# Seven half-size block products in place of eight, in both matrix products of the MLP

## The chip, the cores and the metric

The kernel runs on one core of a Trainium2 chip. The metric is device time in microseconds (us). The five engines work side by side, each through a queue of its own: PE (TensorE) multiplies matrices, DVE (VectorE), ACT (ScalarE) and POOL (GpSimd) work on elements, SP (SyncE) issues all DMAs of this kernel.

## The reference, cut to what matters

Two layers stand one after the other; each is a mixer and an MLP, with norms around both. x is 1024 tokens by 1024 features in float32.

```python
def rmsnorm(x, w, eps=1e-6):
    return x * rsqrt(mean(x * x, axis=-1, keepdims=True) + eps) * w

for layer in range(2):
    x = x + rmsnorm(mixer(rmsnorm(x, mix_pre[layer])), mix_post[layer])
    u = rmsnorm(x, mlp_pre[layer])
    h = square(relu(u @ mlp_w_up[layer]))            # 1024 x 1024 by 1024 x 4096
    x = x + rmsnorm(h @ mlp_w_down[layer], mlp_post[layer])   # 1024 x 4096 by 4096 x 1024
```

Layer 0 mixes by a gated delta rule and an RWKV-7 recurrence, layer 1 by chunkwise retention; the change leaves both mixers as they are.

## The kernel before

A float32 operand of a product is kept as an exact pair of float32r parts, hi = a cast of it on ACT and lo = the rest, by a subtraction on DVE or POOL (`split_w`, `split_act`). A block product is then three matmuls: hi by hi, lo by hi, hi by lo. All matmuls go through `mm` (L178); those of the MLP stream 512 columns each.

`mlp` works in three stages. In the first (L1187 to L1210 and L1252 to L1258), `normed(t)` does the norms for token tile t of 128 tokens: `post_norm` (a load of the residual, `rms`, a POOL product with the norm's weights at L250, a DVE step at L252), then `pre_norm` (`rms` again, L259) and the transposes on PE (L265), whose results are split into the pair `us[hf]` of a half of 512 tokens. `mlp` is a generator: its first steps run between the last products of the mixer. `upward` (L1214) makes feature tiles of the hidden layer, with all of the first half first: 24 matmuls into one PSUM bank for each half and tile, then relu and square on ACT and DVE into hi and lo, which stay in SBUF. So the first half's products can run while the second half's norms are still under way. `downward` (L1233) multiplies two or four of these tiles with their rows of the second weights, 8 token tiles by 2 column halves, and DVE adds each bank to the sum `facc` (L1248). The main loop alternates the two: 15 turns, each of two feature tiles up and two down. At the end, the last `downward` goes token tile by token tile with four feature tiles each, and `finish(t)` does the closing norms of a tile (and, in layer 0, those of the next mixer's input) behind it.

SBUF is cut by hand into pieces (`region((a, b))` in kilobytes; a new use of a piece waits for the end of the old). A ring of buffers (`area(n)`) holds n tiles of a name. The order on each engine is set by the order of the code and by a scheduler's clock; what it gave is quoted with the change.

## Time and profile before

| | |
|---|---|
| time, median of 3 runs | 3415.32 us (3414.01 to 3421.27) |
| the profiled execution: its span | 3408.8 us, which is 6.5 us under the median |
| PE busy in the span | 3265.6 us (96%), 17192 matmuls |
| DVE, ACT, POOL busy | 1845.1 (54%), 1053.1 (31%), 682.8 us (20%) |
| mean granted clock of PE | 0.957 of full speed |

The profile gives no time of its own for the profiled execution beside its span, so the span and the 6.5 us around it stand for it. A busy time is a sum over stages with different limits. Stage by stage it reads otherwise: in the mixers every engine works in turns, and in the MLPs PE has hardly a gap. The views used below are the page's summary; the busy time of each engine by stretch of the span; the groups of instructions by line and shape; and the instructions of one engine in order of time, with the wait before them in brackets.

### The profile page before, as it was taken

The numbers are of one execution on the slowest core, as the hardware profiler recorded it, in microseconds if no ns is written. First come the engines' busy times: TensorE is split into PE (matmuls) and PEld (weight loads), VectorE is DVE, ScalarE is ACT, GpSimd is POOL, SyncE is SP. The second block draws the span as 40 slices with busy tenths as digits, with TensorE's granted clock in tenths as the row PEclk, the third lists the DMA queues.
The fourth block names the chain that finished last, engine by engine and source line by source line (L and its number), as shares of the span: only waits on it lengthen the run. The fifth ranks groups of instructions, "written<-read, shape, count | busy, mean of one in ns | idle before, by whom it ended". The sixth has DMA issues, their size and how long they took to land.

```text
span 3408.8 us, 44062 instructions
## 1 busy us (share of the span) xinstructions
PE 3265.6 (96%) x17192; PEld 2789.7 (82%) x17192; DVE 1845.1 (54%) x3539; ACT 1053.1 (31%) x1972; POOL 682.8 (20%) x1217
## 2 busy tenths in 40 slices
PE   8899899999898899999999999999999999999998
PEld 6677788778777788888887899988999888888887
DVE  6445555555544634444448665667656734444445
ACT  5332333232232421121214343234433432222122
POOL 1663364446320200000003101112011200000002
PEclk9898899898696999999999999999999999999999
DMA  5221222121242511111115322344223411111112
GB/s 164 65 62 42 67 71 70 50 68 51 58 146 76 190 45 49 44 49 45 45 48 177 89 85 83 93 128 127 83 85 99 155 44 50 50 50 50 50 50 99
DMA packets 340562, 268.49 MB, mean 79 GB/s; under 512 B 63232, under 2 KB 305792, under 8 KB 340352
## 3 DMA queue, kind: packets, MB, share of 16 engines
q1 hardware_dynamic: 340352, 265.67, 25.9%
q8 instruction: 135, 2.21, 0.3%
q14 instruction: 75, 0.61, 0.1%
HBM read 230.49 MB, written 35.13 MB: 78 GB/s over the span
## 4 chain that ended last, share of the span: by engine, by line
PE 74%; DMA 7%; DVE 7%; POOL 6%; issue 2%; ACT 2%; SPq 1%; DVEq 0%; POOLq 0%; ACTq 0%
PE bank L178 73%; POOL piece L617 3%; POOL piece L613 3%; DMA piece<-dm 2%; DMA dx<-piece 1%; DVE piece L252 1%; DVE piece L198 1%; ACT piece L233 1%; DVE mt L239 1%; DMA piece<-dx 1%; DMA piece<-h 1%; DVE piece L259 1%; DMA piece<-ud 0%; DMA piece<-yd 0%; DVE piece L1248 0%
## 5 line engine op out<-in xcount | busy, mean ns | idle before, releaser
L178 PE MATMUL bank<-piece,piece 128*128 128x512 f32 (+7 forms) x16176 | 3156.1, 357 | 78.9 <-ACT piece L305 15.1
L178 PEld LDWEIGHTS bank<-piece,piece 128*128 128x128 f32 (+1 forms) x16176 | 2666.3, 196 | 530.6 <-issue 33.6
L1248 DVE TENSOR_TENSOR piece<-piece,bank 128x512 f32<-128x512 f32 x448 | 307.1, 686 | 523.0 <-PE bank L178 521.1
L198 DVE TENSOR_TENSOR piece<-piece,piece 128x1024 fp32r<-128x1024 f32 x322 | 406.7, 1263 | 261.2 <-ACT piece L197 253.9
L197 ACT CAST piece<-piece 128x1024 fp32r<-128x1024 f32 x332 | 347.8, 1048 | 477.4 <-PE bank L178 383.4
L250 POOL TENSOR_TENSOR piece<-piece,piece 128x1024 f32<-128x1024 f32 x32 | 81.2, 2539 | 1618.1 <-DVE piece L1248 1329.4
L1225 ACT ACTIVATE piece<-bank 128x512 f32<-128x512 f32 x128 | 76.3, 596 | 735.2 <-PE bank L178 735.2
L613 POOL TENSOR_TENSOR piece<-piece 128x120 f32<-128x120 f32 (+22 forms) x496 | 182.7, 368 | 219.5 <-DMA piece<-dm 184.0
L617 POOL TENSOR_TENSOR piece<-piece,piece 128x120 f32<-128x120 f32 (+22 forms) x496 | 194.5, 392 | 37.4
L1331 POOL TENSOR_TENSOR piece<-piece,piece 128x512 f32<-128x512 f32 x32 | 64.1, 2004 | 521.7 <-DVE piece L1330 467.2
L305 ACT CAST piece<-piece 128x256 fp32r<-128x256 f32 (+3 forms) x122 | 65.9, 545 | 174.9 <-DVE piece L1500 40.2
L1227 DVE TENSOR_TENSOR piece<-piece 128x512 f32<-128x512 f32 x128 | 89.8, 702 | 52.6 <-ACT piece L1226 52.5
L306 DVE TENSOR_TENSOR piece<-piece,piece 128x256 fp32r<-128x256 f32 (+3 forms) x122 | 82.6, 684 | 53.2 <-ACT piece L305 39.2
L233 ACT ACTIVATE piece<-piece 128x1024 f32<-128x1024 f32 (+1 forms) x64 | 67.7, 1057 | 110.0 <-DVE piece L1248 56.1
L1226 ACT ACTIVATE piece<-piece 128x512 fp32r<-128x512 f32 x128 | 80.9, 632 | 47.1 <-PE bank L178 44.9
L1228 DVE TENSOR_TENSOR piece<-piece,piece 128x512 fp32r<-128x512 f32 x128 | 90.1, 704 | 1.6
L178 PE MATMUL bank<-piece 64*128 64x128 f32 (+1 forms) x384 | 61.3, 315 | 9.1 <-DVE piece L979 7.1
L660 DVE COPY_PREDICATED piece<-piece,bank 128x384 f32<-128x384 uint32 (+2 forms) x96 | 41.9, 440 | 51.8 <-PE bank L178 51.4
L265 PE MATMUL bank<-ident,piece 128*128 128x128 f32 x256 | 41.1, 306 | 28.7 <-DVE piece L259 24.6
L178 PEld LDWEIGHTS bank<-piece 64*128 64x128 f32 (+1 forms) x384 | 53.0, 216 | 17.1 <-DVE piece L979 8.6
L638 DVE STREAM_TRANSPOSE piece<-piece 128x256 f32<-128x256 f32 x16 | 7.1, 445 | 107.4 <-DMA piece<-dx 96.8
L265 PEld LDWEIGHTS bank<-ident,piece 128*128 128x128 f32 x256 | 34.0, 158 | 36.4 <-DVE piece L259 26.5
(191 smaller groups left out, 1713.7 us busy)
## 6 DMA issues: line engine op xcount, KB each, us to landing
piece<-in_ret_w_in_dram SPq DMA_DIRECT2D x96, 512.0 KB
piece<-in_mlp_w_up_dram SPq DMA_DIRECT2D x64, 512.0 KB
piece<-in_mlp_w_down_dram SPq DMA_DIRECT2D x64, 512.0 KB
piece<-in_ab_w_in_dram SPq DMA_DIRECT2D x60, 512.0 KB
piece<-in_ret_w_out_dram SPq DMA_DIRECT2D x32, 512.0 KB
h<-piece SPq DMA_DIRECT2D x24, 512.0 KB
piece<-h SPq DMA_DIRECT2D x24, 512.0 KB
piece<-in_x_dram SPq DMA_DIRECT2D x16, 512.0 KB
```

Source lines behind the costliest of these rows:

```text
L178: PE.matmul(ps, lhsT, rhs, start=start, stop=stop)
L197: ACT.copy(hi, raw)
L198: eng.tensor_tensor(out=lo, in0=raw, in1=hi, op=ALU.subtract)
L233: ACT.activation(junk, xt, AF.Square, accum_out=ss)
L250: POOL.tensor_tensor(out=u, in0=f, in1=wb, op=ALU.mult)
L306: DVE.tensor_tensor(out=lo, in0=y, in1=hi, op=ALU.subtract)
L613: POOL.tensor_tensor(out=t, in0=Mb[:, j : j + 1, j + 1 : 32].to_broadcast([P, c, n]), in1=X[:, 0:c, j : j + 1].to_broadcast([P, c, n]), op ...
L617: POOL.tensor_tensor(out=X[:, 0:c, j + 1 : 32], in0=X[:, 0:c, j + 1 : 32], in1=t, op=ALU.subtract)
L1226: ACT.activation(hH[:, sl], r, AF.Square)
L1227: DVE.tensor_tensor(out=r, in0=r, in1=r, op=ALU.mult)
L1228: DVE.tensor_tensor(out=hL[:, sl], in0=r, in1=hH[:, sl], op=ALU.subtract)
L1248: DVE.tensor_tensor(out=dstf, in0=dstf, in1=ps, op=ALU.add)
```

## The change

Both products of each MLP are done by the Strassen-Winograd scheme. Each operand is cut in four blocks, sums of blocks are formed, seven block products are made, and their sums give the four blocks of the result.

Upward (16 steps p per layer, each for two feature tiles): the blocks of the weights are a11, a12, a21, a22 (feature tile by half of the 1024 inputs), those of the normed input b11, b21 (first token half) and b12, b22 (second). t1 = b12 - b11, t2 = b22 - t1, t3 = b22 - b12, t4 = b21 - t2 are formed once, in `combine(t)`, as the second half's transposes come out. Each step forms four sums of the weights on POOL, splits seven operands, and makes seven products of 12 matmuls. Where two products go into a sum together, the second is added to the first in its PSUM bank, so a step uses four banks. Relu is on ACT, the square on POOL, and the squared tile goes to DRAM (`store`).

Downward (4 quarters c of the hidden layer per layer, 7 products n each, two steps s to a product): the raw blocks of hidden layer and weights are loaded (`fetch`), POOL forms the sums (`prepare`), ACT and DVE split them into a ring of three, PE makes 24 matmuls a step into four banks, and `flush` adds a bank to one of seven accumulators (ACT copies it in quarter 0). In quarter 3, `combined` adds the accumulators into `facc`, and `end` starts the closing norms behind the last two products.

```diff
@@ first stage: the second half's operands
+                def sink(g, ps):
...
+                    if g == 0:
+                        ts["b12"] = mk(tp, sh, "b12")
+                        ts["t1"] = mk(tmp, sh, "t1")
+                        ACT.copy(ts["b12"], ps)
+                        DVE.tensor_tensor(out=ts["t1"], in0=ps, in1=b11[0][:, :, tt], op=ALU.subtract)
+                        DVE.tensor_tensor(out=ts["t1"], in0=ts["t1"], in1=b11[1][:, :, tt], op=ALU.subtract)
+                        put("t1", ts["t1"], DVE)
+                        return
...
+                    DVE.tensor_tensor(out=ts["t2"], in0=ps, in1=ts["t1"], op=ALU.subtract)
+                    DVE.tensor_tensor(out=ts["t3"], in0=ps, in1=ts["b12"], op=ALU.subtract)
+                    put("b22", ps, DVE)
+                    put("t2", ts["t2"], DVE)
+                    POOL.tensor_tensor(out=ts["t4"], in0=b21[0][:, :, tt], in1=ts["t2"], op=ALU.subtract)
+                    put("t3", ts["t3"], POOL)
+                    POOL.tensor_tensor(out=ts["t4"], in0=ts["t4"], in1=b21[1][:, :, tt], op=ALU.add)
+                    put("t4", ts["t4"], POOL)
@@ upward
-            def upward(*tiles, between=()):
...
+            raws = region((0, 16)).area(2)
+            def product(ps, w, u, start, stop):
+                for k in range(4):
+                    PE.matmul(ps, w[0][:, k, :], u[0][:, k, :], start=start and k == 0, stop=False, skip_group_check=True)
+                    PE.matmul(ps, w[0][:, k, :], u[1][:, k, :], start=False, stop=False, skip_group_check=True)
+                    PE.matmul(ps, w[1][:, k, :], u[0][:, k, :], start=False, stop=stop and k == 3, skip_group_check=True)
+            def store(p, f, t, r):
+                POOL.tensor_tensor(out=r, in0=r, in1=r, op=ALU.mult)
+                SP.dma_start(hd[p // 4][f, t][:, p % 4, :], r)
...
+            parts = [first_part(p, begun[p][0], begun[p][1], begun[p][2], keep) for p in range(2)]
+            for p in range(2):
+                second_part(p, parts[p][0], begun[p][2], keep)
+            for p in range(16):
...
+                POOL.tensor_tensor(out=S[:, 0], in0=q["a21"], in1=q["a22"], op=ALU.add)
+                POOL.tensor_tensor(out=S[:, 1], in0=S[:, 0], in1=q["a11"], op=ALU.subtract)
+                POOL.tensor_tensor(out=S[:, 2], in0=q["a11"], in1=q["a21"], op=ALU.subtract)
+                POOL.tensor_tensor(out=S[:, 3], in0=q["a12"], in1=S[:, 1], op=ALU.subtract)
+                b6 = mk(psu, [P, HT], "pu")
+                product(b6, operand(S[:, 1]), ops["t2"], True, True)
+                u2 = mk(us_, [P, HT], "u2")
+                DVE.tensor_tensor(out=u2, in0=x1, in1=b6, op=ALU.add)
...
@@ downward
-            def downward(i0, hs, after=None):
...
+            half = region((24, 32)).area(1)
+            ring = region((104, 136), (40, 56)).area(3)
+            def prepare(n, s, v):
+                if n == 7:
+                    a, b = mk(half, sh, "s3"), mk(half, sh, "t3")
+                    plus(POOL, a, v["a11"], v["a21"], ALU.subtract)
+                    plus(POOL, b, v["b22"], v["b12"], ALU.subtract)
+                elif n == 5:
+                    a, b = v["a21"], v["b12"]
+                    plus(POOL, a, a, v["a22"])
+                    plus(POOL, b, b, v["b11"], ALU.subtract)
+                elif n == 6:
+                    a, b = v["a21"], v["b12"]
+                    plus(POOL, a, a, v["a11"], ALU.subtract)
+                    plus(POOL, b, v["b22"], b, ALU.subtract)
+                elif n == 3:
+                    a, b = v["a12"], v["b22"]
+                    plus(POOL, a, a, v["a21"], ALU.subtract)
+                elif n == 4:
+                    a, b = v["a22"], v["b12"]
+                    plus(POOL, b, b, v["b21"], ALU.subtract)
...
+                return split_in(ring, sh, a, "a"), split_in(ring, sh, b, "b")
+            def combined(n):
+                for t in range(4):
+                    v = {k: x[t] for k, x in acc.items()}
+                    if n == 7:
+                        plus(POOL, v[4], v[7], v[4], ALU.subtract)
+                    elif n == 1:
+                        plus(POOL, v[2], v[2], v[1])
+                    elif n == 5:
+                        plus(POOL, v[3], v[3], v[5])
+                        plus(POOL, v[5], v[5], v[7])
+                    elif n == 6:
+                        plus(DVE, v[1], v[1], v[6])
+                        plus(DVE, v[3], v[3], v[1])
+                        plus(DVE, v[4], v[4], v[1])
+                        plus(POOL, v[5], v[5], v[1])
+            order = (7, 1, 5, 6, 2, 3, 4)
```

Three places show how the instructions now stand. In the names, the number behind `piece` is where the buffer lies in kilobytes, and the number behind `bank` is the PSUM bank.

PE, layer 0, around the last transposes of the first stage (`L265` before, `L267` after). Before:

```order
L178 MATMUL bank6_7_75<-piece164_40_7660,piece40_53_7977 128x512
L178 MATMUL bank6_7_75<-piece148_38_7658,piece56_55_7979 128x512
L265 MATMUL bank2_3_71<-ident_59_127,piece72_51_7706 128x128 x4
L265 MATMUL bank3_4_72<-ident_59_127,piece72_51_7706 128x128 x4
L265 MATMUL bank1_2_70<-ident_59_127,piece72_51_7706 128x128 x4
L178 MATMUL bank4_5_73<-piece172_41_7661,piece88_46_7669 128x512
L178 MATMUL bank5_6_74<-piece172_41_7661,piece40_53_7977 128x512
L178 MATMUL bank0_1_69<-piece172_41_7661,piece48_54_7978 128x512
L265 MATMUL bank2_3_71<-ident_59_127,piece72_51_7706 128x128 x4
```

After, with the first and the last two of the eight groups of transposes:

```order
L1290 MATMUL bank1_2_70<-piece164_40_7676,piece40_48_7996 128x512
L1291 MATMUL bank1_2_70<-piece156_39_7675,piece56_50_7998 128x512
L267 MATMUL bank3_4_72<-ident_75_143,piece172_43_7681 128x128 x4
L267 MATMUL bank2_3_71<-ident_75_143,piece172_43_7681 128x128 x4
...
L267 MATMUL bank2_3_71<-ident_75_143,piece172_43_7681 128x128 x4
L1289 MATMUL bank6_7_75<-piece104_52_8013,piece48_49_7997 128x512
L1290 MATMUL bank6_7_75<-piece112_53_8014,piece48_49_7997 128x512
L1291 MATMUL bank6_7_75<-piece104_52_8013,piece64_51_7999 128x512
```

Before, the second half's transposes stand among the first half's products; now all eight groups stand together behind the 48 matmuls of the two early products of p = 0 and 1, and the next product (with t2, piece 104) stands behind all of them.

POOL, layer 0, the same place: L250 and L1178 are the norms' product with their weights, L198 the split of weights, L1248, L1250 and L1227 the work of `combine` on t3 (piece 196) and t4 (piece 24, piece 96), L1298 a square, L1338 and L1340 the first sums of weights. Before:

```order
L250 TENSOR_TENSOR piece120_50_7677<-piece104_47_7672,piece196_45_7665 128x1024 x4
L198 TENSOR_TENSOR piece56_55_7979<-piece36_8_151,piece40_53_7977 128x1024
L250 TENSOR_TENSOR piece120_50_7677<-piece104_47_7672,piece196_45_7665 128x1024 x2
L198 TENSOR_TENSOR piece64_56_7980<-piece36_8_151,piece48_54_7978 128x1024
L198 TENSOR_TENSOR piece88_46_7669<-piece32_7_150,piece88_46_7669 128x1024
L250 TENSOR_TENSOR piece120_50_7677<-piece104_47_7672,piece196_45_7665 128x1024 x2
```

After:

```order
L1178 TENSOR_TENSOR piece172_43_7681<-piece172_43_7681,piece32_41_7677 128x1024 x6
L1298 TENSOR_TENSOR piece16_63_8184<-piece16_63_8184 128x512 x2
L1248 TENSOR_TENSOR piece24_62_8023<-piece156_39_7675,piece24_62_8023 128x512
L1250 TENSOR_TENSOR piece24_62_8023<-piece24_62_8023,piece164_40_7676 128x512
L1227 TENSOR_TENSOR piece196_57_8018<-piece24_62_8023,piece188_56_8017 128x4x128
L1178 TENSOR_TENSOR piece172_43_7681<-piece172_43_7681,piece32_41_7677 128x1024
L1227 TENSOR_TENSOR piece96_61_8022<-piece24_62_8023,piece88_60_8021 128x4x128
...
L1227 TENSOR_TENSOR piece96_61_8022<-piece24_62_8023,piece88_60_8021 128x4x128
L1338 TENSOR_TENSOR piece24_64_8229<-piece0_46_7993 128x512
L1340 TENSOR_TENSOR piece24_64_8229<-piece0_46_7993 128x512
```

The norms of the last two token tiles now stand behind the squares of p = 0 and 1, which wait for the early products, and the first sums of weights stand behind all of `combine`, whose scratch (piece 24) they take over.

POOL, layer 0, end of the MLP: pieces 72 to 96 are `facc`, 16 and 64 accumulators 7 and 1, the 128x1024 rows `prepare`, L1178 and L250 the closing norms. Before:

```order
L198 TENSOR_TENSOR piece56_55_7979<-piece32_7_150,piece40_53_7977 128x1024
L250 TENSOR_TENSOR piece120_71_11683<-piece72_61_8328,piece104_69_11640 128x1024 x2
L250 TENSOR_TENSOR piece120_71_11683<-piece80_62_8329,piece104_69_11640 128x1024 x2
```

After:

```order
L1400 TENSOR_TENSOR piece8_71_10106<-piece8_71_10106,piece180_75_10110 128x1024 x2
L1400 TENSOR_TENSOR piece72_76_10127<-piece72_76_10127,piece88_78_10129 128x512 x2
L1400 TENSOR_TENSOR piece80_77_10128<-piece80_77_10128,piece96_79_10130 128x512 x2
L1400 TENSOR_TENSOR piece88_78_10129<-piece88_78_10129,piece16_80_10131 128x512
L1400 TENSOR_TENSOR piece164_72_10107<-piece164_72_10107,piece148_69_10104 128x1024
L1400 TENSOR_TENSOR piece88_78_10129<-piece88_78_10129,piece16_80_10131 128x512
L1400 TENSOR_TENSOR piece96_79_10130<-piece96_79_10130,piece16_80_10131 128x512 x2
L1400 TENSOR_TENSOR piece164_72_10107<-piece164_72_10107,piece148_69_10104 128x1024
L1400 TENSOR_TENSOR piece88_78_10129<-piece88_78_10129,piece64_82_10133 128x512 x2
L1400 TENSOR_TENSOR piece96_79_10130<-piece96_79_10130,piece64_82_10133 128x512 x2
L1178 TENSOR_TENSOR piece72_76_10127<-piece72_76_10127,piece0_94_11879 128x1024 x2
```

Before, POOL does nothing in the MLP but the norms at its two ends; now the sums of accumulators stand between `prepare` for product 4 and the two rows of product 3 (piece 164), which PE needs.

## Rows read from the trace of the kernel before

**Rows 1.** The page's summary: span, and busy time, share and instructions by engine.

```profile
span 3408.8 us, 44062 instructions
PE 3265.6 (96%) x17192; PEld 2789.7 (82%) x17192; DVE 1845.1 (54%) x3539; ACT 1053.1 (31%) x1972; POOL 682.8 (20%) x1217
```

**Rows 2.** Busy time (count) by engine, clock, DMA share, GB/s; one stretch per MLP.

```profile
1400.00:1500.00 100.00, 100.00 (x443) 82.87 (x442) 47.76 (x65) 21.09 (x29) 0.00 (x0) 1.00 0.20 61
3200.00:3300.00 100.00, 100.00 (x443) 82.84 (x442) 45.72 (x64) 17.63 (x24) 0.00 (x0) 1.00 0.14 43
```

**Rows 3.** ACT in order of time (start, length), the same relu one loop turn apart.

```profile
1305.14 0.60 ACT L1225 ACTIVATE piece<-bank 128x512 f32<-128x512 f32 x1 [14.72 <-PE bank L178]
...
1348.66 0.60 ACT L1225 ACTIVATE piece<-bank 128x512 f32<-128x512 f32 x1 [14.72 <-PE bank L178]
```

**Rows 4.** DVE in groups by line and shape: busy us, mean ns, idle before.

```profile
L1248 DVE TENSOR_TENSOR piece<-piece,bank 128x512 f32<-128x512 f32 x448 | 307.1, 686 | 523.0 <-PE bank L178 521.1
L1228 DVE TENSOR_TENSOR piece<-piece,piece 128x512 fp32r<-128x512 f32 x128 | 90.1, 704 | 1.6
```

**Rows 5.** DVE in order of time: a 1024-wide subtraction and a norm's step, POOL idle.

```profile
1107.73 1.22 DVE L198 TENSOR_TENSOR piece<-piece,piece 128x1024 fp32r<-128x1024 f32 x1
1108.88 1.28 DVE L252 SCALAR_TENSOR_TENSOR piece<-piece,mr,piece 128x1024 f32<-128x1024 f32 x1
```

**Rows 6.** POOL in order of time: a sum 512 wide.

```profile
1870.34 1.30 POOL L1413 TENSOR_TENSOR piece<-piece,piece 128x512 fp32r<-128x512 f32 x1 [0.73 <-ACT piece L1412]
```

**Rows 7.** ACT in groups by line and shape: casts 1024 wide.

```profile
L197 ACT CAST piece<-piece 128x1024 fp32r<-128x1024 f32 x332 | 347.8, 1048 | 477.4 <-PE bank L178 383.4 <-DMA piece<-in_mlp_w_up_dram 65.4 <-DMA piece<-in_ret_w_in_dram 9.7
```

**Rows 8.** POOL in order of time: first stage of the MLP of layer 0.

```profile
1130.96 4.76 POOL L198 TENSOR_TENSOR piece<-piece,piece 128x1024 fp32r<-128x1024 f32 x2
```

**Rows 9.** DVE in order of time, there: three steps on one column each.

```profile
1131.06 2.31 DVE L240 SCALAR_TENSOR_TENSOR mt<-mt,ms 128x1 f32<-128x1 f32 x1
1133.41 2.33 DVE L241 SCALAR_TENSOR_TENSOR mr<-mt,mr 128x1 f32<-128x1 f32 x1
...
1141.69 0.16 DVE L240 SCALAR_TENSOR_TENSOR mt<-mt,ms 128x1 f32<-128x1 f32 x1
```

**Rows 10.** POOL in order of time: a closing norm's product in layer 0.

```profile
1825.40 2.42 POOL L250 TENSOR_TENSOR piece<-piece,piece 128x1024 f32<-128x1024 f32 x1 [3.93 <-DVE piece L252]
```

**Rows 11.** DVE in order of time, there: a step that reads a PSUM bank.

```profile
1826.42 0.68 DVE L1248 TENSOR_TENSOR piece<-piece,bank 128x512 f32<-128x512 f32 x1
```

**Rows 12.** PE in order of time: first stage in layer 0, from its first longer run.

```profile
1126.95 13.24 PE L178 MATMUL bank<-piece,piece 128*128 128x512 f32 x50 [3.27 <-DVE piece L281]
...
1142.12 5.27 PE L178 MATMUL bank<-piece,piece 128*128 128x512 f32 x22
...
1151.66 6.91 PE L178 MATMUL bank<-piece,piece 128*128 128x512 f32 x22 [2.36 <-POOL piece L198]
...
1164.89 75.39 PE L178 MATMUL bank<-piece,piece 128*128 128x512 f32 x329
```

**Rows 13.** ACT in order of time: the last token tile's first norm in layer 1.

```profile
2701.79 1.06 ACT L233 ACTIVATE piece<-piece 128x1024 bf16<-128x1024 f32 x1 [2.96 <-DVE piece L1363]
```

**Rows 14.** Busy time by stretch, as rows 2: first stage and end of both MLPs.

```profile
2700.00:2720.00 20.00, 18.18 (x89) 14.87 (x88) 19.06 (x32) 11.22 (x21) 7.06 (x3) 1.00 0.54 181
2720.00:2740.00 20.00, 20.00 (x94) 16.66 (x93) 8.22 (x13) 5.89 (x10) 0.00 (x0) 1.00 0.23 79
...
3390.00:3409.00 19.00, 9.79 (x44) 7.77 (x42) 9.91 (x22) 4.33 (x9) 7.14 (x3) 0.81 0.44 166
```

**Rows 15.** The same, the turn from layer 0 to layer 1.

```profile
1800.00:1850.00 50.00, 46.85 (x221) 37.28 (x219) 45.49 (x89) 24.86 (x50) 17.35 (x7) 1.00 0.45 154
1850.00:1870.00 20.00, 16.84 (x79) 14.37 (x80) 17.38 (x34) 7.47 (x15) 7.10 (x4) 0.83 0.75 247
```

**Rows 16.** POOL in order of time: the last two closing norms of layer 1.

```profile
3395.54 2.40 POOL L250 TENSOR_TENSOR piece<-piece,piece 128x1024 f32<-128x1024 f32 x1 [3.01 <-DVE piece L1248]
3400.94 2.34 POOL L250 TENSOR_TENSOR piece<-piece,piece 128x1024 f32<-128x1024 f32 x1 [3.00 <-DVE piece L1248]
```

More of the change, by code (lines that the diff above doesn't have):

```diff
@@ L1252, in mlp @@
-            if layer == 0:
-                for t in (4, 5, 4):
-                    next(run[t])
-                steps = ((6, 5, 4), (7, 6, 5), (7, 6), (7,))
-            else:
-                steps = ((7, 6), (7,))
-            hs = upward(0, 1, 2, 3, between=steps)
-            facc = [mk(fp, [P, D], f"fa{t}") for t in range(8)]
-            downward(0, hs[:2])
-            prev = (2, hs[2:])
-            for g in range(2, 15):
-                hs = upward(2 * g) + upward(2 * g + 1)
-                downward(*prev)
-                prev = (2 * g, hs)
@@ L1281, in mlp, with quads, operand @@
-            run = [finish(t) for t in range(8)]
-            def after(t):
+            def quads(p):
+                raw = mk(raws, [P, KT, 2 * P], "raw")
+                SP.dma_start(raw, mlp_w_up[layer][:, 2 * P * p : 2 * P * (p + 1)].rearrange("(k p) c -> p k c", p=P))
+                return {f"a{f + 1}{k + 1}": raw[:, 4 * k : 4 * k + 4, P * f : P * f + P] for f in range(2) for k in range(2)}
+            def operand(src, eng=DVE):
+                return split_in(ring, [P, 4, P], src, "op", eng)
```

253 lines of the change are left out of this document (183 added, 70 removed).

## The prediction

> **What bounds the kernel now.** The summary comes first: PE is busy for 96% of the span, no other engine for more than 54% [rows 1]. That is a mean over stages, so the next view is the busy time by stretch. In the middle of either MLP, PE is busy for 100.00 of 100 us at the full granted clock, while DVE stands at 46 to 48 and ACT at 18 to 21, and POOL does nothing at all [rows 2]. The same relu comes back after 1348.66 - 1305.14 = 43.52 us [rows 3]; that is a turn of the main loop, with 96 matmuls up (two feature tiles, two halves, 24 each) and 96 down. So one matmul costs 43.52 / 192 = 0.2267 us, and in this stage every matmul less is worth that, as long as PE stays the engine that is waited for. What has to be asked is who keeps PE fed, since the three others are given more to do, and POOL most.
>
> **What the change removes.** Each MLP has 2 x 1536 matmuls before (32 feature tiles x 2 halves x 24 up; 32 x 16 x 3 down). Seven eighths are left, 2688: 16 steps x 7 x 12 = 1344 up, 4 quarters x 7 x 48 = 1344 down. Over both layers 768 matmuls go, of the same shape: 768 x 0.2267 = **-174.1 us**. The Trainium skill, on the page "TensorE: Matmul & The Clock Gate", section "Wait — 56ns, not 53.3ns?", has 215.7 ns between such matmuls, with which the term would be 165.7; the trace has 226.7 here, weight loads included, and that is used.
>
> **What it adds, and whom DVE and POOL wait for.** The new work has one price that a sum of busy times does not show. Two POOL subtractions took 4.76 us from 1130.96 on [rows 8]; in that time DVE steps on a single column, 0.16 us long at other times, took 2.31 and 2.33 us [rows 9]: each had to wait for the POOL instruction under way. Both their inputs lie in SBUF. A DVE step that reads a PSUM bank kept its 0.68 us under a POOL product [rows 10, 11]. So POOL's work on SBUF and DVE's steps with two SBUF inputs take turns, and I add them up: "the shared sum". The Trainium skill says the same, on "SBUF — State Buffer", section "Who interferes with whom": an exclusive lock, and only for DVE instructions with two SBUF inputs; by that rule the bank sums stay free, and if they did not, the last rival below would be the forecast. Prices: DVE 1.22 us for 1024 columns, 1.28 for a norm's step [rows 5], 0.70 for 512, 0.69 from a bank [rows 4]; POOL 2.40 for 1024 [rows 16], 1.30 for 512 [rows 6]; ACT 1.05 for 1024 [rows 7].
>
> *Upward, steady.* A step has 84 matmuls, 19.0 us. POOL: four sums and four squares, 8 x 1.30 = 10.4. DVE: seven splits, 4.9, and five sums from banks, 3.4. Shared sum 15.3, DVE 8.3, ACT twelve instructions of about 0.6 [rows 3], 7.2. All are under 19.0, and the ring holds six to eight operands, which is at least 16 us of PE ahead. Cost nothing; PE is the cover, and if a step became bound by the shared sum it would have to grow by 3.7 us first.
>
> *Downward, quarters 0 to 2.* A quarter has 336 matmuls, 76.2 us. POOL: 16 instructions of `prepare`, 38.4. DVE: 28 splits, 34.2; 28 flushes, 19.3 (on ACT in quarter 0). Shared sum 72.6, only 3.6 us under PE; the ring lets a split run two steps (10.9 us) ahead. Product 6 needs sums in place over product 5's, so POOL works in bursts with the splits between. I take 1.5 us of stall a quarter, six quarters: +9 (0 if the ring covers all; 5 a quarter if it does not: 0 to 30). The loads (8 MB a quarter, about 110 GB/s) are under the 181 GB/s that one 20 us stretch moved [rows 14].
>
> *Quarter 3.* `combined` adds 20 POOL sums, 26.0 us, and 12 DVE sums with both inputs in SBUF, 8.4. Shared sum 72.6 + 34.4 = 107.0, against 76.2 + 10.9 of lead. Of the 20 over, the last four POOL sums (5.2) stand behind both rows of product 3, so PE does not wait for them: 15, rounded to +16 for a layer, +32 in all (24 to 40; half of it if the order leaves more room: 16).
>
> *First stage, layer 0.* Only two of a step's seven products need the first token half alone, so PE has 4 x 12 = 48 matmuls, 10.9 us, while the second half's norms run; before it had 96, and more after them. In the quoted order all transposes of the second half stand behind the 48, and the product with t2 behind all transposes. From 1126.95 [rows 12] the 48 end at 1137.8. Then follow on POOL: two squares 2.6, the last two norms' products 4.8, 16 instructions of `combine` 20.8, three sums of weights 3.9: 32.1; and DVE's part with two SBUF inputs: 12 x 0.70 + 4 x 1.28 = 13.5. That is 45.6, with a split behind it about 47; some DVE steps will lie ahead, so the product starts at about 1180. PE idles 42 us. Before, 99 matmuls (22.4 us) stood in the 38 us from 1126.95 to where the long run sets in [rows 12], so 16 were lost already: **+26** (12 if only the last tile's own chain counts, 40 if DVE's bank steps add up with it).
>
> *First stage, layer 1.* `raws` lies at 0 to 16 KB, where the mixer's last outputs are read, so the weights of p = 0 can be loaded only after them; the last tile's norm starts at 2701.8 [rows 13], a load of 1 MB at 181 GB/s [rows 14] takes about 6, and the 48 matmuls start at about 2709. DVE then has 28 steps of `combine`, 19.3, six splits 4.2, two norm steps 2.6, and about 5 of waits for POOL, from the first transposes at 2712: the t2 product starts at about 2743. PE loses 2743 - 2701 - 11 = 31. Before, 1.8 us were idle in that time [rows 14], and by estimate 4 went to transposes: +25 (10 to 35).
>
> *Clock.* After PE's idle time at the turn of the layers, a stretch of 20 us shows a granted clock of 0.83 [rows 15], which is 3.4 us lost between the full 2.4 and 1.2 GHz. Two long idle times are new: +6 (2 to 8).
>
> *Up to down.* a11 and a21 take the place of b11, which is free 6 products, 16 us, before the end; 2 MB, and one sum and split, just fit in: +2 a layer, +4 (0 to 14).
>
> *Ends.* Before, tiles reach the closing norm 5.4 us apart [rows 16]; now the last four come within 4.1 us, and POOL and DVE need 4 x (2.40 + 1.28) = 14.7 for them. PE's 44 matmuls end at about 3400 [rows 14], 8.8 us before the end; then it would be about 16: +8 (3 to 14). At the turn to layer 1, 3.2 + 3.2 us were idle already [rows 15]; eight norms now crowd there too, each with two norm steps: +8 (0 to 20).
>
> Sum: 9 + 32 + 26 + 25 + 6 + 4 + 8 + 8 = 118 given back of 174: **-56 us**. The span of 3408.8 would become 3353, and with the 6.5 us around it, at which the profiled execution stands below the median of 3415.3, **3359 us**.
>
> **The rivals.** *A: little is given back.* The added work hides and PE stays full, as in the middle of the MLPs now [rows 2]. For it: every steady sum above is under PE's time. Against it: the quoted order puts the transposes behind the 48 matmuls. With the low ends 0 + 16 + 12 + 10 + 2 + 0 + 3 + 0 = 43: 3415 - 131 = 3284.
>
> *B: slower, because the downward half is bound by DVE and POOL together.* If POOL's bursts stop DVE in its queue so that the flushes behind a waiting split wait too, POOL and all of DVE add up: 38.4 + 34.2 + 19.3 = 91.9 in quarters 1 and 2, 15.7 over PE each; in quarter 3 126.3, 39 over PE with its lead. That is 2 x (31.4 + 39) = 141 where I have 41: 3459. It decides against the change once a quarter takes about 14 us longer than forecast in each of the four (8 x 7 = 56, with the last one double). For it: 4 to 6 us of the four flushes stand between splits; DVE is a queue in order. Against it: flushes run in just the time in which a split would wait for POOL [rows 10, 11], and product 1 and 2 have no sums at all.
>
> That the change does not do what it says is no rival: the two orders differ by exactly 768 matmuls, 15483 to 14715 PE instructions.
>
> **How the numbers follow.** Forecast, with its own range of 3305 to 3405: 0.72. A, down to 3280: 0.14. B, above 3410: 0.14. The range takes in A's middle and leaves out about half of A's tail and B: 3280 to 3410. A measurement of this kernel can tell about 0.2% from no change, so faster means below 3408.5 and slower above 3422: 0.83, 0.03 and 0.14.
>
> **What would show it.** Right: PE's matmuls are 768 fewer and a run of 336 takes 76 to 78 us in quarters 0 to 2; two gaps of 35 to 45 us at the t2 products, with DVE and POOL taking turns in them; a stall of some 15 us in quarter 3 before product 3, ended by POOL. Wrong: gaps in the upward steps; quarters over 85 us (B); the second half's operands ready within 20 us of the early products (A); a load from DRAM as the releaser of a downward step.

## The result: 3447.4 us, one per cent slower

The changed kernel takes 3447.44 us (median of four runs, 3436.65 to 3458.76), the kernel before 3418.3 in the same series: 1.0107 times as long, with an interval of 1.0066 to 1.0149. The forecast was 3359 with a range up to 3410. The profiled run of the changed kernel took 3436.65, of which 3434.9 are its span, 10.8 us under its median; its span is 26.1 us over that of before [rows 1].

Lines of the changed kernel's code have numbers of their own: L1289 to L1291 are the matmuls upward and L1491 to L1493 downward, L235 a norm's square, L1178 its product with the weight row on POOL, L1179 and L261 the last steps of the first and of the second norm, L1176 and L1180 the load and the store of a residual row, L267 the transposes, L1169 the cast and L1170 the remainder of a split, L1227 a remainder in `combine`, L1400 a sum downward.

The page's summary answers [rows 1]: 768 matmuls fewer and 151.9 us less work for PE, more than twice the work for POOL.

```profile
span 3434.9 us, 44170 instructions
PE 3113.7 (91%) x16424; PEld 2653.9 (77%) x16424; DVE 2153.4 (63%) x3555; ACT 1255.8 (37%) x2252; POOL 1498.0 (44%) x1665
```

The busy time by stretch, for the steady upward half, the closing quarter 3 of layer 0 and the first stage of layer 0 (columns as in [rows 2]):

```profile
1400.00:1500.00 100.00, 100.00 (x443) 82.81 (x442) 43.21 (x61) 37.39 (x62) 46.87 (x40) 1.00 0.36 117
...
1752.00:1850.00 98.00, 82.84 (x336) 66.34 (x334) 92.18 (x80) 32.89 (x38) 78.06 (x34) 0.90 0.10 32
...
1112.00:1219.00 107.00, 26.59 (x117) 20.35 (x116) 66.81 (x121) 41.53 (x82) 42.01 (x26) 0.60 0.39 134
```

In the middle all is as forecast: PE is full, POOL at 47% hides. In quarter 3 DVE is busy for 92 of 98 us; its waits for POOL count as busy there. In the first stage PE worked 27 of 107 us, at a mean granted clock of 0.60, and no engine was full. DVE's 66.81 and POOL's 42.01 us together would fill the 107, so this row alone does not tell a shared sum of work from a chain. The view of the chain that ended last speaks for a chain (its longest pieces: start, length, what), and e1 below decides it:

```profile
1118.13 7.96 DMA piece<-fd
1126.11 2.19 ACT piece L235 x4
1130.19 1.28 DVE piece L1179
1131.47 1.21 DVE piece L261
1132.72 1.98 PE bank L267 x8
1134.72 3.92 DMA piece<-fd
1138.66 2.19 ACT piece L235 x4
1142.74 1.28 DVE piece L1179
1144.02 1.21 DVE piece L261
1145.28 1.98 PE bank L267 x8
1147.28 3.98 DMA piece<-fd
```

A tile's transposes end, the next row of the mixer's output is loaded into the buffer that they left, then two norms, then transposes: 12.6 us a tile, one tile at a time, although the ring holds two. The 48 early matmuls start at 1159.7, 46.9 us after the mixer's last matmul (4.1 in the kernel before), the product with t2 at 1218.8 (PE in order of time):

```profile
1159.68 1.22 PE L1289 MATMUL bank<-piece,piece 128*128 128x512 f32 x2
...
1218.82 0.79 PE L1289 MATMUL bank<-piece,piece 128*128 128x512 f32 x1 [10.89 <-ACT piece L1169]
```

At the end the same: SyncE's queue in order of time, and DVE's last steps of the norms.

```profile
3399.91 2.38 SPq L1180 DMA_DIRECT2D out_dram<-piece  x2
3402.58 2.66 SPq L1176 DMA_DIRECT2D piece<-h  x2
3410.25 4.46 SPq L1180 DMA_DIRECT2D out_dram<-piece  x2
3414.81 2.84 SPq L1176 DMA_DIRECT2D piece<-h  x2
3420.52 2.16 SPq L1180 DMA_DIRECT2D out_dram<-piece  x2
3423.20 2.36 SPq L1176 DMA_DIRECT2D piece<-h  x2
3428.36 2.72 SPq L1180 DMA_DIRECT2D out_dram<-piece  x2
```

```profile
3419.21 1.28 DVE L1179 SCALAR_TENSOR_TENSOR piece<-piece,mr,piece 128x1024 f32<-128x1024 f32 x1 [1.53 <-DMA piece<-h]
...
3427.05 1.28 DVE L1179 SCALAR_TENSOR_TENSOR piece<-piece,mr,piece 128x1024 f32<-128x1024 f32 x1 [4.74 <-DMA piece<-h]
```

Two stores, two loads, two stores: a pair of residual rows is loaded only when the pair before has been stored. The last matmul ends at 3397.6, 37.3 us before the end; before it was 9.0.

**Where the time went.** A stage's loss is the time between two marks, less 0.2267 us for each matmul of an MLP in it; its excess is that minus the same in the kernel before. That kernel has no quarters; what it lost itself between its last downward matmuls, 8.5 us, is taken off at the turn, where the forecast counted it too, and the loss of quarter 3 stands in full. The marks are matmuls: the 5000th of the mixer of layer 0 (at 1066.7 before, 1066.0 after), the first of each quarter, the last downward, the 1000th and 5000th of the mixer of layer 1, and the end. Excess in us; the columns e1 to e13 are experiments told below, quarters are of both layers together:

| | forecast | changed | e1 | e2 | e3 | e5 | e8 | e13 |
|---|---|---|---|---|---|---|---|---|
| first stage, layer 0 | 26 + 3 | 68.1 | 33.2 | 68.9 | 73.4 | 33.4 | 32.4 | 28.9 |
| first stage, layer 1 | 25 + 3 | 34.4 | 35.3 | 35.3 | 33.8 | 34.1 | 38.3 | 34.6 |
| quarters 0 to 2 | 9 + 4 | 12.3 | 10.7 | 12.9 | 12.4 | 13.8 | 13.7 | 17.3 |
| quarter 3 | 32 | 43.4 | 43.9 | 42.6 | 31.4 | 28.0 | 28.3 | 25.9 |
| turn to layer 1 | 8 | 15.2 | 13.6 | 11.4 | 18.8 | 15.0 | 14.3 | 12.4 |
| end | 8 | 28.2 | 26.1 | 17.0 | 33.2 | 19.8 | 12.0 | 12.7 |

(The forecast's 6 for the clock stand with the first stages, its 4 for up to down with the quarters.) In the changed kernel that is 201.6, the mixers took 1.5 less, and -174.1 + 200.1 = +26.0 is the difference of the spans. Where an edit does not touch a stage, its loss still varies by 3 to 5 us from profile to profile. In the first stage of layer 0 that scatter lies in the end of the mixer, from its 5000th to its last matmul (44 to 51 us in the 15 profiles). From the mixer's last matmul to the product with t2 the four kernels that leave this stage as it is (changed, e2, e3, e7) take 106.0 to 107.0 us; in layer 1 the same four take 44.5 to 46.0.

### The profile page after: what moved, and what is told of

Same layout as the page of the kernel before. It is cut to its first block, busy times and chain, and to the rows that moved or that the text cites. A ratio compares the mean times of both kernels' runs of the same rounds, so it can differ in the third digit from the quotient of the medians.

```text
span 3434.9 us, 44170 instructions
## 1 busy us (share of the span) xinstructions
PE 3113.7 (91%) x16424; PEld 2653.9 (77%) x16424; DVE 2153.4 (63%) x3555; ACT 1255.8 (37%) x2252; POOL 1498.0 (44%) x1665
## 4 chain that ended last, share of the span: by engine, by line
PE 58%; DVE 12%; POOL 11%; DMA 10%; issue 5%; ACT 2%; SPq 1%; DVEq 0%; POOLq 0%; ACTq 0%
PE bank L180 33%; PE bank L1290 5%; PE bank L1291 5%; PE bank L1289 5%; POOL piece L1400 4%; POOL piece L619 3%; DVE piece L1170 3%; POOL piece L615 3%; PE bank L1492 2%; PE bank L1493 2%; PE bank L1491 2%; DVE piece L1400 2%; DMA piece<-dm 2%; DMA dx<-piece 2%; DMA piece<-h 1%
## 5 line engine op out<-in xcount | busy, mean ns | idle before, releaser
L180 PE MATMUL bank<-piece,piece 128*128 128x512 f32 (+7 forms) x10032 | 1742.2, 335 | 70.5 <-ACT piece L307 19.1
L180 PEld LDWEIGHTS bank<-piece,piece 128*128 128x128 f32 (+1 forms) x10032 | 1501.2, 199 | 279.3 <-issue 35.8
L1170 DVE TENSOR_TENSOR piece<-piece,piece 128x512 fp32r<-128x512 f32 (+1 forms) x448 | 643.3, 1454 | 190.4 <-ACT piece L1169 185.8
L1169 ACT CAST piece<-piece 128x512 fp32r<-128x512 f32 (+1 forms) x448 | 365.4, 836 | 701.1 <-PE bank L1290 248.2
L1400 POOL TENSOR_TENSOR piece<-piece,piece 128x1024 f32<-128x1024 f32 (+1 forms) x168 | 471.3, 2835 | 175.5 <-DVE piece L1170 69.0
L1492 PE MATMUL bank<-piece,piece 128*128 128x512 f32 x896 | 353.9, 395 | 30.5 <-DVE piece L1170 30.5
L1289 PE MATMUL bank<-piece,piece 128*128 128x512 f32 x896 | 351.5, 393 | 19.5 <-ACT piece L1169 16.8
L1491 PE MATMUL bank<-piece,piece 128*128 128x512 f32 x896 | 350.7, 395 | 9.1 <-ACT piece L1169 9.1
L1290 PE MATMUL bank<-piece,piece 128*128 128x512 f32 x896 | 350.5, 391 | 1.9 <-DVE piece L1227 1.9
L1493 PE MATMUL bank<-piece,piece 128*128 128x512 f32 x896 | 351.3, 393 | 0.3 <-DVE piece L1170 0.3
L1291 PE MATMUL bank<-piece,piece 128*128 128x512 f32 x896 | 350.0, 391 | 0.1
L200 DVE TENSOR_TENSOR piece<-piece,piece 128x1024 fp32r<-128x1024 f32 x202 | 261.8, 1297 | 136.4 <-ACT piece L199 133.7
L199 ACT CAST piece<-piece 128x1024 fp32r<-128x1024 f32 x204 | 213.5, 1047 | 300.0 <-PE bank L180 274.2
L1492 PEld LDWEIGHTS bank<-piece,piece 128*128 128x128 f32 x896 | 170.4, 190 | 71.7 <-DVE piece L1170 36.5
L1289 PEld LDWEIGHTS bank<-piece,piece 128*128 128x128 f32 x896 | 169.6, 189 | 56.4 <-ACT piece L1169 17.4
L1491 PEld LDWEIGHTS bank<-piece,piece 128*128 128x128 f32 x896 | 170.6, 191 | 47.2 <-ACT piece L1169 11.2
L1290 PEld LDWEIGHTS bank<-piece,piece 128*128 128x128 f32 x896 | 169.7, 189 | 37.8 <-DVE piece L1227 2.4
L1493 PEld LDWEIGHTS bank<-piece,piece 128*128 128x128 f32 x896 | 170.5, 190 | 36.0 <-DVE piece L1170 0.8
L1291 PEld LDWEIGHTS bank<-piece,piece 128*128 128x128 f32 x896 | 169.3, 189 | 36.8 <-DVE piece L1170 1.5
```

What stands on the lines that cost most here:

```text
L180: PE.matmul(ps, lhsT, rhs, start=start, stop=stop)
L1169: ACT.copy(hi, src)
L1170: eng.tensor_tensor(out=lo, in0=src, in1=hi, op=ALU.subtract)
L1289: PE.matmul(ps, w[0][:, k, :], u[0][:, k, :], start=start and k == 0, stop=False, skip_group_check=True)
L1290: PE.matmul(ps, w[0][:, k, :], u[1][:, k, :], start=False, stop=False, skip_group_check=True)
L1291: PE.matmul(ps, w[1][:, k, :], u[0][:, k, :], start=False, stop=stop and k == 3, skip_group_check=True)
```

## The experiments

**e1, buffers and order in the first stage of layer 0.**

```diff
-                nfa = region((172, 180)).area(2)
...
+                early = region((104, 120)).area(4), region((120, 136)).area(4)
+                mid_ = region((172, 180)).area(2), region((180, 188)).area(2)
+                late_ = region((56, 64)).area(2), region((64, 72)).area(2)
...
-                steps = ((0, 1, 0, 0, 2, 1), (1, 3, 2), (2, 4, 3), (3, 5), (4, 5))
+                steps = ((0, 1, 2, 3, 0, 1), (0, 1, 2, 3), (2, 3, 4), (5, 4), (6, 5))
```

> The first stage of layer 0 alone is changed: each of the eight token tiles gets a buffer of its own for the mixer's output and one for the residual rows (space that the operands of the second half take later), and the first four tiles' loads and norms are asked for before their transposes. No arithmetic is added or taken away. Theory R (rings): in the changed kernel each tile there takes 12.6 us (transposes at 1132.7, 1145.3, 1157.9) because one tile's load, norms and transposes must end before the next one's load lands, so this stage falls from 67 us over the kernel before to 25 to 35, and the run to 3400 to 3412. Theory S (shared sum of POOL and DVE): the work of both engines is what takes the time, none of it is gone, so the run stays within 8 us of 3447.

3399.2 us, ratio 0.9981 [0.9953, 1.0008]; the stage's excess falls from 68.1 to 33.2 and every other stage stays. PE in order of time shows the first half's transposes:

```profile
1110.43 1.10 PE L267 MATMUL bank<-ident,piece 128*128 128x128 f32 x8 [3.52 <-DVE piece L261]
1114.78 1.97 PE L267 MATMUL bank<-ident,piece 128*128 128x128 f32 x8 [3.25 <-DVE piece L261]
1117.09 1.12 PE L267 MATMUL bank<-ident,piece 128*128 128x128 f32 x4 [0.34 <-DVE piece L283]
1119.19 1.12 PE L267 MATMUL bank<-ident,piece 128*128 128x128 f32 x4 [0.99 <-DVE piece L283]
1124.75 1.97 PE L267 MATMUL bank<-ident,piece 128*128 128x128 f32 x8 [4.44 <-DVE piece L261]
```

Four tiles in 16 us, where it was 47 (1112.7 to 1159.9). Theory R holds: with no instruction less on PE, DVE, ACT or POOL, 35 us come back.

**e9, the order alone**, with `steps = ((0, 1, 0, 1, 0, 1), (2, 3, 2, 3), (2, 3, 4), (5, 4), (5,))` and rings of two.

> The changed kernel with the order of the first stage's steps in layer 0 changed and nothing else, rings of two as they are: tiles 0 and 1, then 2 and 3 are asked for in pairs, a tile's second norm and transposes ahead of the next pair's loads. Theory O (order): the 12.6 us a tile come from a second norm that stands behind the next tile's first in the queues of ACT and DVE, while that tile's rows wait for a free buffer; two tiles then go in 12.6 us or a little more, and the stage falls by 20 to 30 of the 35 that buffers and order together gave: ratio to the kernel before 1.001 to 1.005. Theory B (buffers): two buffers with a load of 4 us behind each pair are the limit whatever the order: the stage within 5 us of before this edit, ratio 1.008 to 1.013.

Ratio 1.0045 [1.0023, 1.0068], the stage 14 us shorter: between the theories. The ratio is what order foretold, the stage's 14 are short of its 20. From the mixer's last matmul to the product with t2 it is 91.8 us where the changed kernel has 106.0 and e1 72.5. So of the 35 this order alone gives 14, and 21 need the buffers.

**e2, more buffers for the closing norms.**

```diff
-                            nrm, rowa = region((16, 24)).area(2), region((0, 8)).area(2)
+                            rowa = region((0, 8)).area(2)
+                            nrm = region((16, 24), (56, 72), (188, 196)).area(8) if layer else region((16, 24), (64, 72)).area(4)
```

> Only the ring of residual rows in the closing norms is changed: eight buffers in layer 1 and four in layer 0 in place of two. Theory R: the last norms come in pairs 8 to 9 us apart (their steps end at 3399.8/3401.9, 3410.2/3414.3, 3420.5/3422.3, 3428.3/3430.7) because a pair's rows are loaded only after the rows of the pair before have been stored; with all rows there the end after the last matmul falls from 37 us to 15 to 20 and the turn to layer 1 gets 5 to 8 shorter: 3447 - 25 = 3415 to 3428. Theory S: four tiles times POOL's 2.4 and DVE's 1.28 and what DVE still has queued set the end: within 8 us of 3447.

Ratio 1.0039 [1.0016, 1.0062]. All eight loads are now issued before the last matmul, which ends at 3389.1: two at 3053, the six others here (SyncE's queue in order of time):

```profile
3358.16 6.36 SPq L1176 DMA_DIRECT2D piece<-h  x4
...
3372.27 0.80 SPq L1176 DMA_DIRECT2D piece<-h  x2
3389.84 21.48 SPq L1180 DMA_DIRECT2D out_dram<-piece  x8
```

The end is 11 us shorter, the turn 4, which is hardly beyond its scatter (13.6 to 18.2 in kernels that leave it alone); forecast were 17 to 22 and 5 to 8. R is right on the cause and too large: with the rows there, what stands next is POOL's products and DVE.

**e3, the closing sums on DVE** (five lines of `combined`, `plus(POOL, ...)` to `plus(DVE, ...)`).

> The 20 sums for each layer that close quarter 3 on POOL (1.3 us each) are done by DVE (0.7 us each); nothing else is changed. Theory S: POOL and DVE with two SBUF inputs take turns, so what counts is the sum of both, and it falls by 20 x 0.6 = 12 us for a layer; quarter 3 (98.4 and 97.4 us, 76.2 if PE were full) gets 8 to 12 us shorter in each layer: 3423 to 3431. Theory Q (queue): DVE's splits stand behind the sums in DVE's own queue, so what POOL gives up DVE has to do before its next split, 14 us more for DVE: no gain, or up to 15 us longer in each layer: 3445 to 3477.

Ratio 1.0088 [1.0056, 1.0121]. Quarter 3 is 7 and 5 us shorter, where S wanted 8 to 12 in each layer; turn and end are 4 and 5 longer, of which the turn's 4 lie within its scatter. PE's waits at product 3 of layer 0 fall from 12.7 to 3.4 us, and a new one of 4.2 stands at product 6. So POOL's sums have their price in quarter 3, and between 5 and 9 of the 12 us gained are lost again at the next place. That DVE comes to the norms later because of the sums that it now has would fit; it is not shown.

**e7, no sums downward.**

> The changed kernel with all sums of the downward half left out (those of the operands and the closing ones of quarter 3; the output is then not the product), everything else as it is: splits, matmuls, flushes, loads, rings. Theory S: the sums on POOL and what DVE waits for them are what PE waits for: quarter 3 loses 0 to 3 us in place of 22 and 21, quarters 0 to 2 under 5 in place of 7.9 and 4.3 for a layer: 3390 to 3405. Rival L: the loads from DRAM and the splits alone hold PE up: more than half of the 55 us stays, 3420 or more.

Ratio 0.9896 [0.9852, 0.9940]. No quarter loses anything (0.3 us in quarter 3 of both layers together); quarter 3 of each layer, by stretch:

```profile
1760.00:1836.00 76.00, 76.00 (x337) 62.86 (x335) 54.11 (x66) 33.20 (x41) 6.08 (x3) 1.00 0.16 49
3278.00:3354.00 76.00, 76.00 (x337) 62.96 (x336) 53.63 (x66) 29.64 (x36) 9.45 (x4) 1.00 0.07 24
```

All 55 us of the quarters' losses are the sums, those on DVE included; loads and splits hide entirely. L falls. The whole time fell further than S had said: 3373.2 us, where it had 3390 to 3405; the end, which S left out, is 6.7 us shorter too.

**e4, the combinations on DVE** (the sums for t4 and the remainders of t3 and t4 in `combine`), and **e14, POOL's part of them left out.**

> In the first stage of both layers the sums for t4 and the rounding remainders of t3 and t4 (16 POOL instructions of 1.3 us for a layer) are done by DVE (0.7 us each); nothing else is changed. Theory S: the sum of both engines falls by 9.6 us for a layer, and the product with t2 starts 7 to 10 us earlier in layer 1, where the two take turns from 2748 to 2772, and up to 6 in layer 0: 3431 to 3440. Theory R: layer 0 is paced by its rings and gains under 2 there; layer 1 gains as under S. Theory Q: DVE gets 11 us more in its queue ahead of the last tile's t2, and layer 1's product starts up to 8 us later: 3447 to 3460.

> The changed kernel with POOL's part of the combinations left out in both first stages: no sums for t4 and no remainders of t3 and t4 (16 POOL instructions of 1.3 us a layer; t4 is a copy of t2, and the products with t3 and t4 read the rounded part twice, so the output is not the product). DVE's own work is the same as before. Theory S: DVE's steps with two SBUF inputs took 1.7 us in place of 0.7 there because POOL was at work, so without these the first stage of layer 1 falls by 8 to 20 us, that of layer 0 by 3 to 10. Theory Q: DVE's own queue sets it, POOL's work fits beside it: both within 3 us. Theory R for layer 0: the rings set its pace and it gains under 4.

e4: ratio 1.0100 [1.0065, 1.0136], first stages 1.5 us longer each. From the mixer's last matmul to the product with t2 it takes 103.1 us in layer 0, 3 less than the four kernels that leave this stage alone, and 49.2 in layer 1, 3 more. So S and R fall in layer 1, where Q has the direction; in layer 0 it is a small gain, which S had allowed. e14: ratio 1.0030 [1.0003, 1.0057], first stages 8.7 (layer 0) and 5.8 us (layer 1) shorter; to the product with t2 93.0 and 41.5 us, 13 and 4 less. A stretch of 20 us in layer 1's first stage, of the changed kernel, of e4 and of e14:

```profile
2740.00:2760.00 20.00, 8.08 (x38) 6.17 (x37) 19.76 (x22) 8.40 (x16) 17.53 (x13) 0.70 0.07 26
```

```profile
2744.00:2764.00 20.00, 7.68 (x38) 5.61 (x36) 20.00 (x28) 9.41 (x18) 10.27 (x8) 0.69 0.25 79
```

```profile
2740.00:2760.00 20.00, 6.65 (x34) 5.12 (x32) 19.82 (x27) 10.79 (x22) 15.36 (x10) 0.74 0.24 79
```

DVE is under way for all of it in each of the three: its queue sets this stage in layer 1. POOL's part costs it 4 to 6 us, less than S wanted; done on DVE, the same work costs as much. In layer 0 R expected under 4 and got 8.7, or 13 by the shorter stretch, so the rings are not all there either. The chain of the changed kernel shows why: ahead of the product with t2 it runs through POOL's own queue, where the sum of weights (L1338) that this product needs stands behind the last of `combine` (L1227, L1250):

```profile
1211.76 1.82 POOL piece L1227
1213.57 1.22 POOL piece L1250
1215.52 1.26 POOL piece L1227
1216.86 1.26 POOL piece L1338
```

In e14 the first three are gone, and PE's wait there is 5.55 us where it was 10.89.

**e5, e1 to e3 together**, and layer 0's weight sums in space of their own (`sums = region((24, 32) if layer else (180, 188)).area()`).

> The changed kernel with three edits of the earlier runs together (own buffers in the first stage of layer 0, more buffers for the closing norms, the closing sums of quarter 3 on DVE), and the weight sums of layer 0's upward half in space of their own, where the changed kernel has them in the space of the last tile's temporaries. Theory R: the edits sit in different stages and add up: 35 + 15 + 12 less, and 3 to 6 for the weight sums, which now need not wait for the last tile: a span of about 3370, a ratio to the kernel before of 0.980 to 0.992. Rival: the stages are tied together by DVE's queue, and what one edit gains the next stage gives back, as the closing sums on DVE did in part (12 us less in quarter 3, 9 more at the turn and the end): ratio 0.993 to 1.0.

3385.1 us, ratio 0.9925 [0.9897, 0.9953]: the ratio lies between the two theories, and its interval reaches into both. The stages tell more: their excesses sum to 144 us, 57 less than in the changed kernel where 65 were expected. So the edits add up in the main; the weight sums give nothing (33.2 and 33.4), and the end is 3 us longer than in e2 alone.

**e8, in addition the closing product on DVE** (`eng.tensor_tensor` with `eng=DVE` in `post_norm_in`).

> As the run with the buffers and sums together, but in the closing norms the product with the weight row (2.4 us on POOL for a tile) is done by DVE (1.2 us). Theory S: with the rows there, POOL's four products and DVE's steps take turns after the last matmul, 4 x (2.4 + 1.28), of which DVE alone needs 4 x 2.5: the end gets 4 to 6 us shorter, the turn 2 to 5. Theory Q: DVE's queue is the bound there already, with the flushes in it: no gain, or up to 5 us longer at either place.

Ratio 0.9897 [0.9859, 0.9936]. The end is 7.8 us shorter, more than S said; the turn 0.7, less than it said.

**e6, the downward half in eight products**, on e5's base: four results, each the sum of two products kept in PSUM, one after the other.

> The same as the run with the buffers and sums together, but the downward half goes by eight block products again: 384 matmuls a quarter in place of 336, no sums of operands, no closing sums, four results kept in PSUM over two products each; the second identity alone is undone, the upward half keeps seven. Theory: the downward identity pays for itself only in part: 2 x 43.5 us of matmuls come back, and the losses of the four quarters (12 + 31), most of the excess at the turn and at the end (together some 25) go: 15 to 45 us slower than with seven. Rival: it does not pay at all, the sums cost as much as the matmuls: equal within 10 us, or faster.

3413.7 us, ratio 1.0011 [0.9985, 1.0038], 29 us over e5 by the ratios, as forecast. Quarters 1 to 3 of layer 1 in one stretch, with POOL all but idle:

```profile
3125.00:3387.00 262.00, 261.53 (x1153) 215.94 (x1151) 151.53 (x165) 100.86 (x111) 11.36 (x5) 1.00 0.24 81
```

87 us of matmuls come back, and the excesses sum to 89 us where e5's sum to 144. So the downward identity (seven products in place of eight) is worth some 30 us against this kernel of eight. But this is not the kernel before: in its quarters, turn and end it loses 27 us more than the kernel before (22 of it in quarter 3, while its turn is 6 shorter). Against the kernel before, the downward identity gives 10 us in e5 (-87.0 + 13.8 + 28.0 + 15.0 + 19.8) and 19 in e8; in the changed kernel it cost 12 more than it gave (-87.0 + 12.3 + 43.4 + 15.2 + 28.2), and the upward one 15.5 more (-87.0 + 68.1 + 34.4).

**e10, four banks for the second half's transposes** (`psn = bank_area(3, 2, 7, 6)`), on e8.

> The kernel with the buffers, the sums and the closing product on DVE, and in it four PSUM banks in place of two for the transposes of the second half in both first stages. Theory T: these transposes wait for the bank of the tile before (three of the four tiles waited 5 to 8 us for a remainder that DVE forms out of a bank), so with four banks the first stages fall by 4 to 10 us each: ratio 0.984 to 0.988 where it was 0.990. Theory Q: DVE is busy all through that time and its queue sets the end; the transposes come earlier, the product with t2 does not: within 3 us, ratio 0.989 to 0.991.

Ratio 0.9907 [0.9883, 0.9930], first stages 32.8 and 39.9 where e8 had 32.4 and 38.3. T falls: in layer 1 PE's wait between the last transposes and the product with t2 is 20.2 us where e8 had 3.5. The transposes come earlier and the product does not, as Q had it.

**e11 and e13, three upward steps begun** ahead of the product with t2, on e8; e12 is e11 with e10's banks. In e11 and e12 the third step's weights took the first step's place in layer 0 before these had been used, so one product there has other weights; e13 has them in order.

```diff
-            parts = [first_part(p, begun[p][0], begun[p][1], begun[p][2], keep) for p in range(2)]
-            for p in range(2):
+            parts = []
+            for p in range(3):
+                if p == 2:
+                    begun[2] = (begun[2], operand(begun[2]["a11"]), operand(begun[2]["a12"]))
+                parts.append(first_part(p, begun[p][0], begun[p][1], begun[p][2], keep))
```

> As the kernel with the closing product on DVE, but three steps of the upward half instead of two do their products with the first token half (72 matmuls instead of 48) ahead of the product with t2, in both layers. Theory C (cover): norms and combinations set when t2 is there, and 24 more matmuls take the place of idle time, 5.4 us a layer: both first stages 4 to 6 us shorter, ratio 0.986 to 0.988. Rival Q: the two operands and the square more push t2 back by as much: no change, ratio 0.989 to 0.991.

> Both of the last two edits, four banks and three steps begun. Theories T and C: the gains add up, 0.981 to 0.985. Theory Q: 0.988 to 0.991.

> The kernel with the closing product on DVE and three steps begun, with the third step's operands formed behind the products of the first (in the earlier run of three steps they took the first step's buffers in layer 0 before these had been read). Theory C (cover): what sets the product with t2 is the norms and combinations, so each step begun ahead of it covers 5.4 us of PE's idle time in each layer: both first stages 3 to 6 us shorter than with two steps begun, ratio to the kernel before 0.985 to 0.988. Theory Q: DVE has four splits and the square's turn more in its queue ahead of t2 and gives it back: 0.989 to 0.992.

Ratios 0.9856 [0.9830, 0.9883], 0.9877 [0.9851, 0.9903] and 0.9880 [0.9846, 0.9914]; first stage of layer 0 in e11 and e13 28.0 and 28.9, after 31.2 to 33.4 in the runs with own buffers and two steps begun, but 35.9 in e12; in layer 1 36.2, 34.6 and 38.6, among those with two (30 to 40). By the ratios e12 is where Q had it, and e13 at the edge between C and Q. C is likely in layer 0, by 3 or 4 of its 5.4 us, though e12 speaks against it, and not shown in layer 1. e13, at 3372.3 us, beats both kernels: 1.2% under before. Its time cannot be told from e8's.

## Why the prediction was wrong, step by step

- **Matmuls, -174.1: right.** 768 fewer; an upward step takes 19.04 us (84 x 0.2267), quarter 1 takes 76.2 in either layer.
- **Upward at no cost: right.** No gap between 1240 and 1515, with POOL at 47%.
- **Quarters 0 to 2, +9, and up to down, +4: right** (12.3 together). The loss sits in quarters 0 and 2; from up to down there is no gap.
- **Quarter 3, +32 (24 to 40): the mechanism right, 43.4 in size.** Product 3 is where PE waits, as forecast, three times in layer 0 (below, PE in order of time), 12.7 us in all; product 7 waits 2.5 at 1760, and the other 7 of the 22.2 are the clock, granted at 0.90 in this stretch (PE busy for 82.84 us with matmuls that take 76.2 at the full clock), which had no term in this step. The lines name ACT and DVE, the two halves of a split; that POOL's sums stood ahead of it is shown by e3, where the waits at product 3 fall to 3.4.

```profile
1814.72 2.08 PE L1491 MATMUL bank<-piece,piece 128*128 128x512 f32 x4 [4.02 <-ACT piece L1169]
...
1823.03 0.80 PE L1492 MATMUL bank<-piece,piece 128*128 128x512 f32 x1 [6.23 <-DVE piece L1170]
...
1832.06 0.50 PE L1492 MATMUL bank<-piece,piece 128*128 128x512 f32 x1 [2.40 <-DVE piece L1170]
```

- **First stage of layer 0, +26 (12 to 40): this is the step that failed; it measured 68.** It let the 48 matmuls start at 1126.95, as in the kernel before [rows 12], and counted only the work behind them. But the change also writes both norms in place, so that a tile holds one of two buffers from its load to its transposes; and a tile's second norm stands behind the next tile's first, as it did before, but now the rows of that tile wait for a buffer. The pace ahead of the 48 was a round trip of load, two norms and transposes for each tile, and they began 46.9 us after the mixer's last matmul, where it had been 4.1. The term that the step did have, 42 us from the 48 to the product with t2, measured 46, of which 15.6 are again a wait for one tile's norms. e1 gave 35 back and left 33; e9 puts 14 of them on the order. That those 33 lie near the 26 + 3 of the sum is in part luck: in e1 the 48 still begin 19.6 us after the mixer, and the product with t2 follows 36.5 behind them.
- **End, +8 (3 to 14): 28. Turn, +8 (0 to 20): 15.** The step counted POOL's and DVE's work for four tiles and left out that eight residual rows go through two buffers, a store and a load for each pair. e2 took 11 and 4 of it, and POOL's product with the weight row, which the step did count, 8 more at the end (e8). Before, tiles came 5.4 us apart [rows 16], and the same two buffers sufficed.
- **First stage of layer 1, +25, with clock 28: 34.** The product with t2 starts 46 us after the mixer's last matmul, where the step had 2743 - 2701 = 42; what holds it is DVE's queue, with POOL's turns a part of it (e14).
- **Rival B** had the direction and not the place: quarter 1 was full and the steady quarters lost 12 us in all. Its threshold was off as well: 8 x 7 = 56 makes it 7 us a quarter, and 14 for the last alone. What decided against the change lies in the first stage of layer 0 and at the end, which no rival had.
- **The range.** The upper ends given sum to 30 + 40 + 40 + 35 + 8 + 14 + 14 + 20 = 201, just what was lost, but that is luck: three terms went past their upper ends (first stage of layer 0 68 against 40, quarter 3 43 against 40, end 28 against 14), and the quarters with up to down lost 12 of their 44. The range, up to 3410, allowed 169 given back. What it lacked is a term for rings: at both places where the sum was missed most, buffers were waited for (e1, e2).

## What to carry to other kernels

When a change makes work crowd that a loop had spread out, sum the engines' work and then, separately, count the round trip of every ring there: buffers in flight, and how long one is held from the load into it to its last reader. Writing in place saves space and lengthens just that hold; 35 of the 200 us lost here were had back with no instruction less. And moving work from POOL to DVE pays only where DVE's own queue has room: 12 us in quarter 3, of which 5 to 9 were lost again behind it, and 8 at the end, but 3 us gained and 3 lost in the two first stages.

## What the runs showed of the hardware that was not expected

- Taking turns costs both sides. In the changed kernel the groups by shape give 2.07 us for a DVE split 1024 wide (1.22 alone, [rows 5]) and 3.13 for a POOL sum (2.40 alone, [rows 16]), while DVE's step from a bank kept its 0.68. With the sums left out (e7) the same 224 splits take 1.22 again:

```profile
L1400 POOL TENSOR_TENSOR piece<-piece,piece 128x1024 f32<-128x1024 f32 x128 | 397.0, 3126 | 167.4 <-DVE piece L1170 69.0 <-DMA piece<-in_mlp_w_down_dram 62.8 <-DMA piece<-hd 27.0
```

```profile
L1170 DVE TENSOR_TENSOR piece<-piece,piece 128x1024 fp32r<-128x1024 f32 x224 | 457.1, 2074 | 84.6 <-ACT piece L1169 80.9 <-PE bank L1290 3.3
L1170 DVE TENSOR_TENSOR piece<-piece,piece 128x512 fp32r<-128x512 f32 x224 | 186.2, 834 | 105.8 <-ACT piece L1169 104.9
L1400 DVE TENSOR_TENSOR piece<-piece,bank 128x512 f32<-128x512 f32 x168 | 107.5, 676 | 0.0
```

  The Trainium skill, "GPSIMD Engine Reference", section "4.1 Engine selection", gives elementwise work to VectorE, GPSIMD being about twice as slow with two inputs. The prices agree (1.30 and 0.70 us for 512 columns); by that rule e4 should have gained in both first stages. It gained 3 us in layer 0 and lost 3 in layer 1, where DVE was under way for 20.00 of 20 us.
- The mixer of layer 0, whose code no edit touches, reached its 5000th matmul between 1060.1 and 1083.1 us in the 15 profiles of the changed kernel and its variants; in e3, with the same order of instructions up to there, it was 6.5 us later than in the changed kernel. The cause stays open. So a gain of 5 us is read from its stage, and in the first stage of layer 0 from the mixer's last matmul on, not from the whole time.
